# Attention state products in plain fp32, one accumulator for both directions, gate preparation among the first pairs

## Chip, core and metric

The kernel runs on one core of a Trainium2 chip. The metric is device time in microseconds from launch to end. The core has five engines with a queue each, which wait for one another through semaphores: PE (TensorE, matrix products into PSUM; its weight loads are listed as PEld), DVE (VectorE), ACT (ScalarE), POOL (GpSimd) and SP, which here only starts transfers. Each engine works through its queue in order, so an instruction that waits holds up all that stand behind it.

## The reference

One encoder block on x of 1024 tokens by 1024 channels. A conditioned RMS norm gives h; one wide projection of h gives q, k, v, z of a gated linear attention with 4 heads (128 key, 256 value channels), the three inputs of a gMLP branch, and two merge gates. Both branches are projected, weighted by the gates, summed, projected, scaled per channel by `gate` (from the condition c), added to x and normalised.

The attention runs forwards and backwards and sums the two. In chunks, cut to what matters:

```python
b = cumsum(log_a) within a chunk
q_t, k_t, k_end = q * exp(b), k * exp(-b), k * exp(b_last - b)
o_intra = (mask * (q_t @ k_t.T)) @ v
state   = exp(b_last) * state + k_end.T @ v        # carried from chunk to chunk
o       = o_intra + q_t @ state_before_this_chunk
...
o = o_fw + o_bw
o = o * rsqrt(mean(o * o) + EPS) * gla_norm_g
y_gla = (o * silu(z)) @ w_br_gla
```

## The kernel before

All large products are exact to about fp32 by splitting: an operand a becomes ah (a cast to fp32r on ScalarE) and al = a - ah (a subtraction on VectorE, `split_w`, L175 and L176), and a @ b becomes three fp32r products ah bh + ah bl + al bh. Small products (scores, transposes, spreading a row over partitions) are plain fp32.

The stages in order of time: norm and first product (to about 100 us), gMLP's spatial part and the values of heads 0 and 1 (to about 190), the pairs (190 to 575), q and k of head 0, the attention (about 610 to 965) with other dense products between, the projection of the attention's output (`ev_ya`, to about 1000), the output projection.

*Pairs.* `pair` computes two column blocks of the projection by seven half-size products (Strassen-like): 84 matmuls of 128x512. It reads two weight blocks `wa` and `wb` (SP's queue, L566 and L567), forms sums on POOL (L570 to L577), splits them, and evacuates with `evac`. It takes nine 4 KB tiles of ring `w` (`w4`, 12 buffers): wa, wb, their sum, and three split pairs ah/al, sh/sl, bh/bl. There are 20 such pairs: `pair_m` (merge gates, tanh), `pair_uz` (two pairs, gMLP; it holds two buffers of ring `h` for u), `pair_z`. Ring `h` (`ht`, 30 buffers of 4 KB) holds the split activations; during the pairs 12 of its buffers are kept parts of h and 16 the sums of the products.

*Two small jobs among the pairs.* `low_rank_weights` loads and splits the small decay weights (POOL's queue, then ScalarE and VectorE). `residual_gate` builds `gate` from eight 512 KB blocks `wgate` (SP's queue, L672), each accumulated on VectorE (L676); it needs ring `h` for the accumulator `gacc`, for each `wg`, and for `bg`. Both stand behind the tenth of 14 source calls, after `pair_uz(3)` and `pair_m(FB_MA, ta_d, 1)`.

*Attention.* For each head there are four units in the order of `SEQ`: backward over the second half of the tokens, backward over the first, forward over the first, forward over the second. `front` computes decays, q and k with their exponentials and the masked scores (the backward half of the scores stays in `atb`, the forward half is merged into it). `gla_ops` scales, transposes and splits k (keh, kel) and splits q (qth, qtl). `body` walks the unit's four token tiles. `next_state` forms k_end.T @ v in PSUM (`pk`, one bank), adds the decayed state (L854) and splits the new state (L858, L859). `mm3` is the split product. A backward step forms q @ state at once and keeps it in `op` (L902). A forward step forms scores @ v plus q @ state in one accumulator, adds the kept `op` on VectorE (L925) and squares for the norm on ScalarE (L926). After four tiles `rsq` gives the norm factors, VectorE scales (L931), TensorE transposes (L936), VectorE multiplies with z (L938).

Ring `q` (`w1`, 8 buffers of 1 KB) holds the states and their splits, ring `s` (`w2`, 16 buffers of 2 KB) the 128x512 tiles.

*Order.* A planner builds each engine's queue: it walks a modelled timeline and always takes the ready instruction of highest priority; priority follows the source, and what is traced within `tc.high_priority(offset=PRI)` (the attention, L989) is moved 4000 places ahead. So the dense products traced beside a head (`dense_v`, `dense_qk`, `load_gg`, `dense_yb`) fill the places where the attention isn't ready. A tile that finds no free buffer in its ring waits for a release.

Of the kernel before, what the change touches and what calls it, by code (L numbers as in the profile page):

```python
# [44 lines left out]
def hybrid_block_kernel(ctx: ExitStack, tc: tile.TileContext, x, wf, wt, wada, wgate, wvr, wst, alpha, abias,  # L45
# [77 lines left out]
    def w4(shape, dtype, name):  # L123
        return hp.tile(shape, dtype, tag="w", bufs=12, name=nm(name))
# [4 lines left out]
    def w1(shape, dtype, name):  # L129
        return hp.tile(shape, dtype, tag="q", bufs=8, name=nm(name))  # L130
# [556 lines left out]
    pair_m(FB_MB, tb_d, 0)  # L687
    pair_m(FB_MB, tb_d, 1)
    pair_uz(0)
    pair_m(FB_MB, tb_d, 2)  # L690
    pair_uz(1)
    pair_m(FB_MB, tb_d, 3)
    pair_uz(2)
    pair_m(FB_MA, ta_d, 0)
    pair_uz(3)
    pair_m(FB_MA, ta_d, 1)
    low_rank_weights()
    residual_gate()
# [115 lines left out]
    def gla_ops(un):  # L814
# [13 lines left out]
        qth = w2([P, 512], F32R, "qth")  # L828
        qtl = w2([P, 512], F32R, "qtl")
        S.copy(qth, qh)  # L830
        V.tensor_tensor(out=qtl, in0=qh, in1=qth.bitcast(F32), op=ALU.subtract)
        un.update(keh=keh, kel=kel, qth=qth, qtl=qtl)
# [10 lines left out]
    def next_state(un, i, vh, vl, st, last):  # L843

        if last:
            return None
        o = slice(i * P, i * P + P)
        pk = pk_()
        mm3(pk[:, 0:HV], un["keh"][:, o], un["kel"][:, o], vh, vl, True, True)
        s = w1([P, HV], F32, "s")  # L850
        if st is None:
            V.tensor_copy(s, pk[:, 0:HV])
        else:
            V.scalar_tensor_tensor(out=s, in0=st[0], scalar=un["dec"][:, i:i + 1], in1=pk[:, 0:HV], op0=ALU.mult,  # L854
                                   op1=ALU.add)
        sh = w1([P, HV], F32R, "sh")
        sl = w1([P, HV], F32R, "sl")
        S.copy(sh, s)  # L858
        V.tensor_tensor(out=sl, in0=s, in1=sh.bitcast(F32), op=ALU.subtract)  # L859
        return s, sh, sl  # L860
# [4 lines left out]
    opart = {}  # L865
# [18 lines left out]
    def body(h, u):  # L884
# [5 lines left out]
        if not fw:  # L890
            for i in (3, 2, 1, 0):
                t = half * 4 + i
                o = slice(i * P, i * P + P)
                vh, vl = split_v(h, t)
                st = state[0]
                if i == 3:
                    op4 = w4([P, 4, HV], F32, "op")
                op = opart[h, t] = op4[:, i, :]
                if st is not None:
                    po = po_()  # L900
                    mm3(po[:, 0:HV], un["qth"][:, o], un["qtl"][:, o], st[1], st[2], True, True)
                    S.copy(op, po[:, 0:HV])  # L902
                state[0] = next_state(un, i, vh, vl, st, t == 0)
            return
# [5 lines left out]
        so = tiny([P, 4], "so", 2)  # L910
        for i in range(4):
# [4 lines left out]
            op = opart[h, t]  # L916
            pf = po_()
            po = pf[:, 0:HV]
            mm3(po, ath[:, o], atl[:, o], vh, vl, True, st is None)
            if st is not None:  # L920
                mm3(po, un["qth"][:, o], un["qtl"][:, o], st[1], st[2], False, True)
            if t == NT - 1:
                S.copy(op, po)
            else:
                V.tensor_tensor(out=op, in0=po, in1=op, op=ALU.add)  # L925
            S.activation(pf[:, HV:2 * HV], op, AF.Square, accum_out=so[:, i:i + 1])  # L926
            state[0] = next_state(un, i, vh, vl, st, t == NT - 1)
        r = rsq(so, 4, 1.0 / HV)
        for i in range(4):
            op = opart[h, half * 4 + i]  # L930
            V.tensor_scalar(op, op, r[:, i:i + 1], None, op0=ALU.mult)  # L931
        tsl = slice(half * 512, half * 512 + 512)
        for j in range(2):
            pt = po_()
            for i in range(4):
                TE.transpose(pt[:, i * P:(i + 1) * P], opart[h, half * 4 + i][:, j * P:(j + 1) * P], ident)  # L936
# [35 lines left out]
    for h in range(HEADS):  # L972
# [11 lines left out]
        else:  # L984
            if h == 2:
                load_gg()
            for j in range(4 * (h - 2), 4 * (h - 2) + 4):
# [226 lines left out]
```

## Time and profile before

| | |
|---|---|
| median of 3 runs | 1127.99 us (1127.13 to 1130.76) |
| the profiled execution, its own time | 1132.89 us |
| its span, first to last instruction | 1131.2 us |
| mean granted TensorE clock | 0.979 |
| instructions | 14327 |
| DMA traffic | 152.30 MB, mean 135 GB/s |

The page first gives the busy time of each engine and its share of the span, then the span in 40 slices of 28.3 us, a digit of tenths for each. PEclk is the clock that TensorE was granted. The chain is followed back from the last instruction, at each step to what released it. In a group of instructions stand line, engine, operation, output<-input, shapes, count, busy time, mean ns of one, idle time ahead and what ended it. The duration of a matmul overlaps with the next one's; the spacing of the starts is what it costs. A plain fp32 matmul shows as two records.

### The profile page before, as it was taken

How to read it: one execution, taken by the hardware profiler on the slowest of the kernel's cores; microseconds unless marked ns; L12 is line 12 of the kernel's file. 1: busy time of each engine (PE TensorE's matmuls, PEld its weight loads, DVE VectorE, ACT ScalarE, POOL GpSimd, SP SyncE). 2: the span in 40 equal slices, each digit the busy share in tenths (PEclk: the TensorE clock that was granted, in tenths of full speed). 3: DMA queues.
4: the chain of work that ended last, by engine and by line, in shares of the span. 5: the costliest groups of instructions: out<-in, count | busy, mean ns of one | idle time of the engine just before them, and what ended most of it. 6: DMA issues, size and time to landing. Idle time of an engine off the chain costs nothing.

```text
span 1131.2 us, 14327 instructions
## 1 busy us (share of the span) xinstructions
PE 1077.1 (95%) x5348; PEld 902.6 (80%) x5348; DVE 695.1 (61%) x1085; ACT 431.3 (38%) x760; POOL 264.3 (23%) x302
## 2 busy tenths in 40 slices
PE   6889999999999999999999988999899998999997
PEld 4768899888888888777788977988688877788886
DVE  5765577348475757565544569755867795764422
ACT  4453324233324232523324355544635453322222
POOL 2211214333343425433402000200200100021510
PEclk9999999999999999999999989999899997999999
DMA  9531235232323232355245411622642436536012
GB/s 357 202 140 52 103 122 182 80 112 103 121 103 121 103 121 93 137 188 176 103 164 218 159 38 38 211 87 84 230 143 94 147 142 205 175 123 242 19 56 93
DMA packets 55575, 152.30 MB, mean 135 GB/s; under 512 B 7279, under 2 KB 15471, under 8 KB 55506
## 3 DMA queue, kind: packets, MB, share of 16 engines
q1 hardware_dynamic: 40898, 102.42, 25.8%
q0 software_dynamic: 14608, 48.97, 11.8%
q8 instruction: 42, 0.69, 0.3%
q14 instruction: 27, 0.22, 0.1%
HBM read 108.37 MB, written 42.99 MB: 134 GB/s over the span
## 4 chain that ended last, share of the span: by engine, by line
PE 78%; DVE 7%; DMA 5%; ACT 3%; issue 2%; POOL 1%; SPq 0%; POOLq 0%; ACTq 0%; DVEq 0%
PE pd L193 5%; PE pd L194 5%; PE pd L195 5%; PE po L547 4%; PE po L548 4%; PE pd L211 4%; PE pd L212 4%; PE po L549 4%; PE pd L213 4%; PE pd L549 3%; PE pd L548 3%; PE pd L547 3%; PE pk L547 3%; PE pd L511 3%; PE pd L512 3%; PE pk L548 3%
## 5 line engine op out<-in xcount | busy, mean ns | idle before, releaser
L221 POOL TENSOR_TENSOR r<-ms,nhalf 128x1 f32<-128x1 f32 (+1 forms) x24 | 20.8, 866 | 236.4 <-DVE ms L220 234.2
L511 PE MATMUL pd<-tvl,hh 128*128 128x256 f32 (+1 forms) x256 | 74.1, 290 | 0.6 <-DVE tvl L176 0.6
L512 PE MATMUL pd<-tvh,hl 128*128 128x256 f32 (+1 forms) x256 | 74.2, 290 | 0.0
L510 PE MATMUL pd<-tvh,hh 128*128 128x256 f32 (+1 forms) x256 | 74.0, 292 | 0.0
L549 PE MATMUL pd<-hh,al 128*128 128x512 f32 x160 | 63.9, 399 | 3.1 <-DVE al L176 3.1
L547 PE MATMUL pd<-hh,ah 128*128 128x512 f32 x160 | 63.0, 393 | 1.6 <-ACT ah L175 1.6
L548 PE MATMUL pd<-hl,ah 128*128 128x512 f32 x160 | 62.9, 393 | 0.0
L570 POOL TENSOR_TENSOR wsum<-wb 128x512 f32<-128x512 f32 x20 | 26.2, 1311 | 121.5 <-DMA wb<-in_wf 108.3
L176 DVE TENSOR_TENSOR al<-wa,ah 128x1024 fp32r<-128x1024 f32 x20 | 47.2, 2360 | 10.6 <-PE po L548 6.8
L193 PE MATMUL pd<-ggh,wh 128*128 128x512 f32 x128 | 51.5, 402 | 1.4 <-ACT wh L175 1.0
L1045 PE MATMUL pd<-gh,wh 128*128 128x512 f32 x128 | 51.0, 398 | 0.9 <-ACT gh L175 0.5
L1046 PE MATMUL pd<-gh,wl 128*128 128x512 f32 x128 | 50.7, 396 | 0.8 <-DVE wl L176 0.8
L194 PE MATMUL pd<-ggl,wh 128*128 128x512 f32 x128 | 50.9, 399 | 0.0
L195 PE MATMUL pd<-ggh,wl 128*128 128x512 f32 x128 | 50.8, 397 | 0.1
L511 PEld LDWEIGHTS pd<-tvl,hh 128*128 128x128 f32 x256 | 49.7, 194 | 1.0 <-DVE tvl L176 0.8
L193 PE MATMUL pd<-hh,wh 128*128 128x512 f32 x128 | 50.2, 392 | 0.0
L194 PE MATMUL pd<-hl,wh 128*128 128x512 f32 x128 | 50.2, 392 | 0.0
L195 PE MATMUL pd<-hh,wl 128*128 128x512 f32 x128 | 50.1, 391 | 0.0
L510 PEld LDWEIGHTS pd<-tvh,hh 128*128 128x128 f32 x256 | 49.5, 195 | 0.2
L512 PEld LDWEIGHTS pd<-tvh,hl 128*128 128x128 f32 x256 | 49.6, 194 | 0.0
L1047 PE MATMUL pd<-gl,wh 128*128 128x512 f32 x128 | 48.9, 392 | 0.0
L212 PE MATMUL pd<-tl,mh 128*128 128x512 f32 x120 | 46.9, 391 | 0.0
(319 smaller groups left out, 3173.3 us busy)
## 6 DMA issues: line engine op xcount, KB each, us to landing
ws<-in_wf SPq DMA_DIRECT2D x24, 512.0 KB, 5.3
ws<-in_wt SPq DMA_DIRECT2D x22, 512.0 KB, 4.4
wa<-in_wf SPq DMA_DIRECT2D x20, 512.0 KB, 3.8
wb<-in_wf SPq DMA_DIRECT2D x20, 512.0 KB, 4.4
wa<-in_wada SPq DMA_DIRECT2D x16, 512.0 KB, 8.7
xn<-in_x SPq DMA_DIRECT2D x8, 512.0 KB, 8.9
sg_d<-sg POOLq DMA_DIRECT2D x16, 256.0 KB, 2.4
vh_d<-vh SPq DMA_DIRECT2D x32, 128.0 KB, 1.9
```

The costliest lines, as they stand in the source:

```text
L193: TE.matmul(acc, lhsT=hi[:, k, :], rhs=x.hi(k, half), start=(k == 0), stop=False)
L194: TE.matmul(acc, lhsT=hi[:, k, :], rhs=x.lo(k, half), start=False, stop=False)
L195: TE.matmul(acc, lhsT=lo[:, k, :], rhs=x.hi(k, half), start=False, stop=(k == KC - 1))
L212: TE.matmul(acc, lhsT=xh, rhs=lo[:, k % 2, :], start=False, stop=False)
L510: TE.matmul(acc, lhsT=H.hi_t(k, t), rhs=hi, start=(k == 0), stop=False)
L511: TE.matmul(acc, lhsT=H.hi_t(k, t), rhs=lo, start=False, stop=False)
L512: TE.matmul(acc, lhsT=H.lo_t(k, t), rhs=hi, start=False, stop=(k == KC - 1))
L547: TE.matmul(acc, lhsT=a, rhs=xh(k), start=(first and k == 0), stop=False, skip_group_check=not first)
L548: TE.matmul(acc, lhsT=a, rhs=xl(k), start=False, stop=False, skip_group_check=not first)
L549: TE.matmul(acc, lhsT=b, rhs=xh(k), start=False, stop=(k == 3), skip_group_check=not first)
L1045: TE.matmul(acc, lhsT=hi[:, k, :], rhs=GO.hi(k, half), start=(k == 0), stop=False)
L1046: TE.matmul(acc, lhsT=lo[:, k, :], rhs=GO.hi(k, half), start=False, stop=False)
```

## The change

State products: q and the state are no longer split. The backward units keep their states (`sbw`), and the forward step adds both directions' products q @ state, each as one plain fp32 matmul, to the accumulator of scores @ v. The accumulator is copied out by ScalarE and squared from PSUM; the scaling by the norm factor moves from VectorE to ScalarE. `op` becomes one tile of a forward unit.

Order: `residual_gate` stands behind the first pair and `low_rank_weights` behind the third; the pairs are rearranged around them. Of the eight `dense_yb`, three instead of four are traced beside head 2 and five beside head 3. Ring `w` has 11 buffers instead of 12, ring `q` 12 instead of 8.

```diff
     def w4(shape, dtype, name):
-        return hp.tile(shape, dtype, tag="w", bufs=12, name=nm(name))
+        return hp.tile(shape, dtype, tag="w", bufs=11, name=nm(name))
...
     def w1(shape, dtype, name):
-        return hp.tile(shape, dtype, tag="q", bufs=8, name=nm(name))
+        return hp.tile(shape, dtype, tag="q", bufs=12, name=nm(name))
...
     pair_m(FB_MB, tb_d, 0)
+    residual_gate()
     pair_m(FB_MB, tb_d, 1)
+    pair_m(FB_MB, tb_d, 2)
+    low_rank_weights()
     pair_uz(0)
-    pair_m(FB_MB, tb_d, 2)
+    pair_m(FB_MB, tb_d, 3)
     pair_uz(1)
-    pair_m(FB_MB, tb_d, 3)
+    pair_m(FB_MA, ta_d, 0)
     pair_uz(2)
-    pair_m(FB_MA, ta_d, 0)
+    pair_m(FB_MA, ta_d, 1)
     pair_uz(3)
-    pair_m(FB_MA, ta_d, 1)
-    low_rank_weights()
-    residual_gate()
     pair_z(0)
...
         V.tensor_tensor(out=q3, in0=q3, in1=e8[:, :, fa:fa + 1].broadcast_to([P, 4, P]), op=ALU.mult)
-        qth = w2([P, 512], F32R, "qth")
-        qtl = w2([P, 512], F32R, "qtl")
-        S.copy(qth, qh)
-        V.tensor_tensor(out=qtl, in0=qh, in1=qth.bitcast(F32), op=ALU.subtract)
-        un.update(keh=keh, kel=kel, qth=qth, qtl=qtl)
+        un.update(keh=keh, kel=kel)
...
-            V.scalar_tensor_tensor(out=s, in0=st[0], scalar=un["dec"][:, i:i + 1], in1=pk[:, 0:HV], op0=ALU.mult,
+            V.scalar_tensor_tensor(out=s, in0=st, scalar=un["dec"][:, i:i + 1], in1=pk[:, 0:HV], op0=ALU.mult,
                                    op1=ALU.add)
-        sh = w1([P, HV], F32R, "sh")
-        sl = w1([P, HV], F32R, "sl")
-        S.copy(sh, s)
-        V.tensor_tensor(out=sl, in0=s, in1=sh.bitcast(F32), op=ALU.subtract)
-        return s, sh, sl
+        return s
...
                 st = state[0]
-                if i == 3:
-                    op4 = w4([P, 4, HV], F32, "op")
-                op = opart[h, t] = op4[:, i, :]
-                if st is not None:
-                    po = po_()
-                    mm3(po[:, 0:HV], un["qth"][:, o], un["qtl"][:, o], st[1], st[2], True, True)
-                    S.copy(op, po[:, 0:HV])
+                sbw[h, t] = st
                 state[0] = next_state(un, i, vh, vl, st, t == 0)
...
+        op = w4([P, 4, HV], F32, "op")
...
-            op = opart[h, t]
             pf = po_()
             po = pf[:, 0:HV]
-            mm3(po, ath[:, o], atl[:, o], vh, vl, True, st is None)
-            if st is not None:
-                mm3(po, un["qth"][:, o], un["qtl"][:, o], st[1], st[2], False, True)
-            if t == NT - 1:
-                S.copy(op, po)
-            else:
-                V.tensor_tensor(out=op, in0=po, in1=op, op=ALU.add)
-            S.activation(pf[:, HV:2 * HV], op, AF.Square, accum_out=so[:, i:i + 1])
+            inter = [(x["qh"][:, o], y) for x, y in ((units[h, 1 - half], sbw[h, t]), (un, st)) if y is not None]
+            mm3(po, ath[:, o], atl[:, o], vh, vl, True, not inter)
+            for n, (q, y) in enumerate(inter):
+                TE.matmul(po, lhsT=q, rhs=y, start=False, stop=(n == len(inter) - 1))
+            S.copy(op[:, i, :], po)
+            S.activation(pf[:, HV:2 * HV], po, AF.Square, accum_out=so[:, i:i + 1])
...
-            op = opart[h, half * 4 + i]
-            V.tensor_scalar(op, op, r[:, i:i + 1], None, op0=ALU.mult)
+            S.activation(op[:, i, :], op[:, i, :], AF.Copy, scale=r[:, i:i + 1])
...
-                TE.transpose(pt[:, i * P:(i + 1) * P], opart[h, half * 4 + i][:, j * P:(j + 1) * P], ident)
+                TE.transpose(pt[:, i * P:(i + 1) * P], op[:, i, j * P:(j + 1) * P], ident)
...
-            for j in range(4 * (h - 2), 4 * (h - 2) + 4):
+            for j in ((0, 1, 2), (3, 4, 5, 6, 7))[h - 2]:
                 dense_yb(j)
```

More of the change, by code (lines that the diff above doesn't have):

```diff
@@ L864, in hybrid_block_kernel @@
     atb = {}
-    opart = {}
+    sbw = {}
     state = [None]
```

## The prediction

> **What bounds the kernel now.** I read the profile page from its top: busy times, slices, chain by engine.
>
> ```profile
> PE 1077.1 (95%) x5348; PEld 902.6 (80%) x5348; DVE 695.1 (61%) x1085; ACT 431.3 (38%) x760; POOL 264.3 (23%) x302
> PEclk9999999999999999999999989999899997999999
> PE 78%; DVE 7%; DMA 5%; ACT 3%; issue 2%; POOL 1%; SPq 0%; POOLq 0%; ACTq 0%; DVEq 0%
> ```
>
> TensorE is busy 95% of a span of 1131.2 us and carries 78% of the chain. So an edit pays only if it takes work from PE or closes one of its holes. The clock row shows that holes also cost time inside "busy": in some slices the granted clock falls. The stage windows find the holes. Their columns are the stretch, its length, busy time of PE, PEld, DVE, ACT and POOL, granted clock, DMA share and GB/s.
>
> ```profile
> 220.00:440.00 220.00, 219.81 (x963) 179.99 (x962) 133.44 (x144) 75.01 (x105) 81.27 (x89) 1.00 0.30 108
> 460.00:520.00 60.00, 52.59 (x212) 41.17 (x211) 36.19 (x36) 20.72 (x26) 22.61 (x24) 0.94 0.50 170
> 660.00:720.00 60.00, 51.15 (x309) 44.30 (x308) 51.34 (x103) 35.41 (x81) 5.64 (x8) 0.89 0.18 62
> 780.00:820.00 40.00, 33.58 (x159) 26.26 (x158) 34.13 (x66) 23.99 (x48) 8.51 (x13) 0.87 0.53 195
> 820.00:920.00 100.00, 100.00 (x531) 85.80 (x530) 75.17 (x139) 44.31 (x93) 12.98 (x22) 1.00 0.41 147
> 920.00:965.00 45.00, 39.61 (x192) 32.64 (x191) 31.44 (x61) 21.24 (x48) 1.57 (x2) 0.85 0.41 139
> ```
>
> The pairs (220 to 440) have no hole. I price a hole as idle time plus length times the missing clock, a little generously where both fall together. 460 to 520, where low-rank weights and gate are prepared: 7.4 + 60 x 0.06 = 11.0 us. The attention: 8.9 + 6.6 = 15.5 us, 6.4 + 5.2 = 11.6 us, 5.4 + 6.8 = 12.2 us, together 39.3 us. From 820 to 920 the attention lies under dense products and costs nothing beyond its PE time. In the first two of its three holes VectorE is busy 51.3 of 60 us and 34.1 of 40 us: there it, not PE, sets the pace. How the third part of a state's split holds PE, the timeline of 668 to 675 shows (start, length, then in brackets the idle time before and its releaser):
>
> ```profile
> 671.04 0.38 PE L836 MATMUL po<-sl,qth 128*128 128x256 f32 x1 [0.38 <-DVE sl L859]
> 673.35 0.58 PE L836 MATMUL po<-sl,qth 128*128 128x256 f32 x1 [1.09 <-DVE sl L859]
> 675.01 0.42 PE L837 MATMUL po<-sh,qtl 128*128 128x256 f32 x1
> ```
>
> PE waits for the low part of the state, and after two such waits a product of that shape lasts 0.42 us instead of the 0.28 us shown below.
>
> **The state products.** One head has 7 backward and 7 forward products of q with a state, 56 in all. Each is now three fp32r products of 128x256 and becomes one fp32 product. No fp32 product of that width is in the trace; its neighbours are 128 wide (chain of waits, 16 records) and 512 wide (4 records). A plain fp32 product makes two records: L811 runs 64 times and has 128. Three rows of the timeline in a dense stretch give the fp32r spacing.
>
> ```profile
> L811 PE MATMUL pm<-qh,b 128*128 128x128 f32 x128 | 19.1, 287 | 1.9 <-DVE b L806 1.7
> 124.41 1.78 PE pm L444 x16
> 519.68 1.72 PE pm L682 x4
> 175.73 0.28 PE L511 MATMUL pd<-tvl,hh 128*128 128x256 f32 x1
> 175.85 0.28 PE L512 MATMUL pd<-tvh,hl 128*128 128x256 f32 x1
> ```
>
> A record takes 1.78 / 16 = 0.111 us at 128 and 1.72 / 4 = 0.43 us at 512, so 0.215 us at 256 by halving the latter: 0.43 us a product. Three fp32r products at 0.12 us take 0.36 us. The edit **adds** 56 x 0.07 = 3.9 us to PE; the ends are 56 x (0.22 - 0.36) = -7.8 us and 56 x (0.86 - 0.36) = +28 us from the two neighbours, and I stay with the halved row because the two agree with a cost linear in width. The Trainium skill, page "FP8 and Floating Point Precision", section "TensorE Precision Notes", counts four passes for true fp32, which speaks against trading three products for one: at 0.12 us a pass it would be 56 x 0.12 = 6.7 us, an estimate that would move the time by 3 us.
>
> What goes is on the two other engines:
>
> ```profile
> L859 DVE TENSOR_TENSOR sl<-s,sh 128x256 fp32r<-128x256 f32 x56 | 23.5, 419 | 6.5 <-ACT sh L858 5.9
> L831 DVE TENSOR_TENSOR qtl<-qh,qth 128x512 fp32r<-128x512 f32 x16 | 10.9, 683 | 1.3 <-ACT qth L830 1.3
> L925 DVE TENSOR_TENSOR op<-po,op 128x256 f32<-128x256 f32 x28 | 11.7, 422 | 9.0 <-PE po L837 8.9
> L931 DVE TENSOR_SCALAR op<-op,r 128x256 f32<-128x256 f32 x32 | 9.3, 355 | 2.7 <-POOL r L221 2.7
> L858 ACT CAST sh<-s 128x256 fp32r<-128x256 f32 x56 | 22.7, 405 | 40.6 <-DVE s L854 31.0 <-DVE s L852 9.4
> L830 ACT CAST qth<-qh 128x512 fp32r<-128x512 f32 x16 | 10.0, 622 | 1.5 <-PE po L836 1.1 <-PE pk L836 0.3
> L902 ACT COPY op<-po 128x256 f32<-128x256 f32 x28 | 10.2, 371 | 17.4 <-PE po L837 15.9 <-DMA y_d<-tb 1.4
> L926 ACT ACTIVATE po<-op 128x256 f32<-128x256 f32 x32 | 12.3, 386 | 18.1 <-DVE op L925 17.9
> ```
>
> VectorE loses the split of the state, the split of q, the sum of both directions and the norm scaling: 23.5 + 10.9 + 11.7 + 9.3 = 55.4 us. ScalarE loses 22.7 + 10.0 + 10.2 = 42.9 us and gains 28 copies of the accumulator (at 0.371 us, L902: 10.4 us) and 32 scalings (at 0.386 us, L926: 12.4 us): 20 us less. The step from one state to its product also gets shorter by a cast (0.41 us) and a subtraction (0.42 us). What is late next is the state itself (L854), which PE already awaits.
>
> ```profile
> PE pk L835 <- DVE s L854: 4.5, 5, 1.6
> PE po L836 <- DVE sl L859: 2.8, 5, 1.1
> ```
>
> How much returns I work out hole by hole. The same four lines in each hole, one row per line where it is largest:
>
> ```profile
> 660.00:720.00 60.00, 5.02 (x12) 0.89 0.18 62
> 660.00:720.00 60.00, 2.72 (x4) 0.89 0.18 62
> 660.00:720.00 60.00, 2.95 (x7) 0.89 0.18 62
> 660.00:720.00 60.00, 2.35 (x8) 0.89 0.18 62
> ```
>
> Here (L859, L831, L925, L931 in this order) 13.0 us of VectorE's 51.3 us go, out of a hole of 15.5 us. Some of it lay under dense products, so I take 9 us. By the share of the three holes I take 5 of 11.6 us for 780 to 820, where GG's split and late weights also hold PE, and 8 of 12.2 us for 920 to 965, where the length of the chain counts, since the dense products that covered it are used up at 919.5 us:
>
> ```profile
> L193 PE MATMUL pd<-ggh,wh x128: 387/390/796, 801.4 to 919.5; 128*128 128x512 f32 x128
> ```
>
> Together **-22 us**. Its ends are -39 us (all holes closed) and 0.
>
> **Norm scaling on ScalarE.** Four scalings now stand as 4 x 0.386 = 1.5 us between the norm and the transposes, for 4 x 0.355 = 1.4 us on VectorE, and behind whatever ScalarE has begun (a cast like L830's, 0.62 us). Eight units: +1 us, between 0 (covered by dense products) and +5 us. The copy and the square of a tile, both on ScalarE, hold the accumulator's bank as long as the sum and the square did: nothing.
>
> **Gate and low-rank preparation earlier.** 460 to 520 loses 11.0 us.
>
> ```profile
> L676 DVE SCALAR_TENSOR_TENSOR gacc<-wg,gsc,gacc 128x1024 f32<-128x1024 f32 x7 | 11.3, 1620 | 11.6 <-DMA wg<-in_wgate 11.6
> 459.83 5.10 DMA sa<-in_abias
> 481.23 4.45 DMA wg<-in_wgate
> 485.77 1.30 DVE gacc L676
> 487.09 18.28 SPq L672 DMA_DIRECT2D wg<-in_wgate  x4
> 505.42 0.41 SPq L566 DMA_DIRECT2D wa<-in_wf  x1
> ```
>
> The eight weight loads go one after the other, each after the last accumulation (4.45 + 1.30 us). VectorE stands 11.6 us in front of them, and four of them hold SP's queue for 18.28 us with the next pair's weights (L566) behind. The reason is room: of 30 large buffers the activations keep 12 and the four sums 16, so two are left for accumulator and weight. Before the first `pair_uz` this is no different; that is why I do not let the 11 us vanish. What is better there is that a `pair_m` gives VectorE less to do. What is new: u's buffers of `pair_uz(0)` come free only behind gate and low-rank weights, and the wait on the 5.1 us load still stands in ScalarE's queue. I take **-2 us**, between -11 and +8 us.
>
> **Buffers.** A pair uses nine of the 4 KB buffers; 12 become 11.
>
> ```profile
> L175 ACT CAST ah<-wa 128x1024 fp32r<-128x1024 f32 x20 | 21.0, 1050 | 53.5 <-PE po L548 42.7 <-DVE fl L176 9.8 <-PE pd L512 1.1
> PE pd L549 <- DVE al L176: 3.1, 4, 1.6
> ```
>
> The next pair's first cast already waits for a buffer that PE gives up (42.7 us in all), so one buffer fewer delays it further. Five of the pair's seven products remain then as cover, and PE waits only 3.1 us for `al` today. I take **+2 us**; the ends are 0 and one product of 12 matmuls in each of 20 pairs, 55 us (219.81 us for 963 of them, 0.23 us each). In the attention one held buffer goes (`op4` of the backward direction), so it is even there. The 1 KB ring grows to 12 for the seven states kept: nothing. `dense_yb(3)` behind head 2's attention instead of before it: these products are cover of lower rank than the attention in either place, so 0, between -6 and +6 us.
>
> **Sum.** 3.9 - 22 + 1 - 2 + 2 = -17.1 us on the profiled execution's own 1132.89 us (span 1131.2 us): 1115.8 us. That execution lay 4.9 us above the median of the runs, 1127.99 us, so I forecast **1111 us**.
>
> **Rivals.**
> *All of it returns.* If VectorE alone makes the holes, 33 of 39 us and 8 of the gate's 11 us return: 3.9 + 1 - 33 - 8 = -36 us, 1092 us. For it: VectorE at 86% in two holes. Against it: late weights and PE's wait for L854 stay.
> *VectorE's time was cover.* The freed time is spent waiting for the state (4.5 us against 2.8 us for the split). Then only the split's waits and their slow clock return, about 6 us, against 3.9 + 1 + 2 us added: 1128.9 us. Against it: the 51.3 of 60 us.
> *The slow clock has another cause than the stalls.* Then only the idle part of the holes answers, 20.7 of 39.3 us, and of my 22 us some 11 return: 1122 us. For it: the gaps shown ahead of the slow product are only 0.38 and 1.09 us. Against it: it fell in all three holes and nowhere from 820 to 920. The Trainium skill, page "TensorE: Matmul & The Clock Gate", section "HAM oscillation — how this bites in real kernels", speaks for this rival: it lets the clock fall only after a gap of more than about 3.4 us, and these gaps are shorter.
> *Slower: the ring of 11.* In the pair stage, which has no hole now, each pair's `al` comes a release later. At half a product, 1.4 us, in 20 pairs it costs 28 instead of 2 us: 1111 + 26 = 1137 us. It outweighs the rest from 1 us per pair on. For it: the 42.7 us. Against it: five products of cover.
> *The move does not do what it says.* Gate loads wait for one buffer as before, and the 11 us only change place: 1113 us, inside the forecast.
>
> **Chances.** Forecast 0.49 (1100 to 1121 us), clock 0.07, all of it 0.17, cover 0.15, ring 0.12. What a measurement of this kernel tells from no change is about 0.3%, 3.4 us. Faster: 0.49 + 0.07 + 0.17 + 0.04 of the cover case = 0.77; same: the other 0.11; slower: 0.12. The range runs from the case of a full return to beyond that of cover, 1091 to 1132 us; the ring case and half of the full return are left out.
>
> **What would show it.** L859, L831, L925 are gone; the state products are 112 records of 128x256 near 0.215 us apart. VectorE falls to about 640 us, ScalarE to about 411 us. The clock in the attention's holes rises above 0.89, 0.87 and 0.85. Wrong would be: pairs with idle PE before `al`, a hole as deep as 11 us beside the early gate loads, or the same holes with PE waiting on L854.

## The result: slower by 0.7%

The changed kernel took **1137.18 us** (median of 4 runs, 1136.27 to 1138.12), the kernel before, run beside it, 1129.38 us (4 runs, 1127.13 to 1131.16): a ratio of **1.0070** with a 95% interval of 1.0046 to 1.0094. The forecast was 1111 us (1091 to 1132). The profiled execution of the changed kernel took 1136.27 us with a span of 1134.6 us, 3.4 us more than the span before. Of all the runs below one single execution, of order_fp32sep, took 2146 us; its ratio leaves it out.

### The profile after

Busy times and the chain by engine, from the page:

```profile
PE 1073.5 (95%) x5292; PEld 898.3 (79%) x5292; DVE 642.6 (57%) x953; ACT 413.5 (36%) x720; POOL 272.0 (24%) x302
PE 80%; DVE 9%; DMA 4%; ACT 4%; issue 2%; POOL 1%; SPq 0%; POOLq 0%; ACTq 0%; DVEq 0%
```

VectorE and ScalarE fell to what was worked out (642.6 and 413.5 us against 640 and 411), and PE's share of the chain rose by two points. What was meant to go, went; the time did not follow. The windows, in the columns of before:

```profile
220.00:440.00 220.00, 212.38 (x909) 170.88 (x908) 127.22 (x141) 76.26 (x105) 87.92 (x95) 0.98 0.31 110
460.00:520.00 60.00, 58.95 (x258) 47.91 (x257) 37.45 (x42) 18.82 (x27) 24.12 (x26) 1.00 0.37 129
660.00:720.00 60.00, 49.77 (x286) 42.68 (x285) 43.52 (x77) 33.82 (x77) 6.00 (x9) 0.89 0.17 61
780.00:820.00 40.00, 28.51 (x150) 23.40 (x148) 28.13 (x48) 25.63 (x56) 7.69 (x12) 0.87 0.49 171
820.00:920.00 100.00, 98.33 (x498) 83.58 (x499) 68.66 (x114) 42.62 (x89) 12.18 (x20) 0.97 0.41 143
920.00:965.00 45.00, 42.55 (x212) 35.50 (x211) 21.08 (x32) 19.26 (x43) 4.28 (x6) 1.00 0.59 204
```

I price holes as the forecast did, idle time plus length times missing clock. The hole of 460 to 520 went from 11.0 to 1.1 us, and one of 12.0 us (7.6 + 220 x 0.02) opened in 220 to 440, where there was none. In the attention the four rows give 16.8, 16.7, 4.7 and 2.5 us, 40.7 together, where before they gave 15.5, 11.6, 0 and 12.2, 39.3 together. VectorE is no longer near its limit in the first two (43.5 of 60 and 28.1 of 40 us), yet they did not shrink. The longest waits of PE:

```profile
PE pm L811 <- DVE b L806: 9.2, 2, 5.6
PE pk L547 <- DVE u L603: 6.1, 13, 1.0
PE pk L831 <- DVE s L850: 5.4, 8, 1.0
...
PE pm L682 <- DVE gacc L676: 4.0, 1, 4.0
```

The waits for the low part of the state are gone, as they must be. In their place stands L811, the scores of the next unit, waiting for that unit's preparation (1.7 us in two waits before, 9.2 us now). The wait for the state itself (L850, L854 before) grew from 4.5 to 5.4 us. The last column of numbers is the longest single wait. The wait of L682 is that of the gate's products, in the new hole of the pair stage.

One more row for each kernel shows that the attention did get faster. L778 is the first product of each of the 16 units' preparation; the answer for this line gives its first and last start. Before:

```profile
L778 PE MATMUL pm<-RT,ST x16: 389/394/497, 619.0 to 913.4; 128*128 128x512 f32 x16
```

After:

```profile
L778 PE MATMUL pm<-RT,ST x16: 387/394/765, 626.1 to 897.1; 128*128 128x512 f32 x16
...
L193 PE MATMUL pd<-ggh,wh x128: 387/389/737, 816.0 to 943.0; 128*128 128x512 f32 x128
```

From the first to the last preparation it is 271.0 us instead of 294.4, some 23 us less. But it starts 7.1 us later, and the yb products on GG (L193) now run from 816.0 to 943.0 us, where before they ran from 801.4 to 919.5. The attention outran the dense products; PE still had their work left, and the idle time stood elsewhere. A shorter chain in one place was no shorter program.

### The profile page after: what moved, and what is told of

Its sections match the earlier page's. It is cut to its first block, busy times and chain, and to the rows that moved or that the text cites. A ratio compares the mean times of both kernels' runs of the same rounds, so it can differ in the third digit from the quotient of the medians.

```text
span 1134.6 us, 14014 instructions
## 1 busy us (share of the span) xinstructions
PE 1073.5 (95%) x5292; PEld 898.3 (79%) x5292; DVE 642.6 (57%) x953; ACT 413.5 (36%) x720; POOL 272.0 (24%) x302
## 4 chain that ended last, share of the span: by engine, by line
PE 80%; DVE 9%; DMA 4%; ACT 4%; issue 2%; POOL 1%; SPq 0%; POOLq 0%; ACTq 0%; DVEq 0%
PE pd L195 5%; PE pd L194 5%; PE pd L193 5%; PE pd L211 4%; PE pd L212 4%; PE po L549 4%; PE po L547 4%; PE po L548 4%; PE pd L213 4%; PE pk L547 3%; PE pd L549 3%; PE pd L511 3%; PE pd L512 3%; PE pd L510 3%; PE pk L549 3%; PE pk L548 3%
## 5 line engine op out<-in xcount | busy, mean ns | idle before, releaser
L221 POOL TENSOR_TENSOR r<-ms,nhalf 128x1 f32<-128x1 f32 (+1 forms) x24 | 20.5, 854 | 191.6 <-DVE ms L220 133.2
L549 PE MATMUL pd<-hh,al 128*128 128x512 f32 x160 | 62.2, 389 | 0.0
L193 PE MATMUL pd<-ggh,wh 128*128 128x512 f32 x128 | 51.6, 403 | 0.0
L850 DVE SCALAR_TENSOR_TENSOR s<-s,dec,pk 128x256 f32<-128x256 f32 x48 | 22.9, 477 | 50.5 <-PE pk L833 50.3
L193 PE MATMUL pd<-hh,wh 128*128 128x512 f32 x128 | 50.0, 390 | 0.0
L570 POOL TENSOR_TENSOR wsum<-wb 128x512 f32<-128x512 f32 x20 | 29.0, 1448 | 86.3 <-PE po L548 38.3
L175 ACT CAST ah<-wa 128x1024 fp32r<-128x1024 f32 x20 | 21.0, 1051 | 73.0 <-PE po L549 50.2
```

The lines of the kernel that those rows point to most:

```text
L193: TE.matmul(acc, lhsT=hi[:, k, :], rhs=x.hi(k, half), start=(k == 0), stop=False)
L549: TE.matmul(acc, lhsT=b, rhs=xh(k), start=False, stop=(k == 3), skip_group_check=not first)
```

## The experiments

All times are medians; each ratio is to the kernel before, run beside the variant on the same chip, and 1% is 11.3 us. "Changed" is the changed kernel.

| kernel | us | ratio (95%) |
|---|---|---|
| changed | 1137.18 | 1.0070 (1.0046 to 1.0094) |
| order_only | 1128.34 | 0.9970 (0.9954 to 0.9986) |
| ring11 | 1128.54 | 0.9982 (0.9961 to 1.0003) |
| att_only | 1142.58 | 1.0084 (1.0059 to 1.0109) |
| after_yb4 | 1136.46 | 1.0034 (1.0017 to 1.0051) |
| order_fp32sep | 1120.21 | 0.9896 (0.9873 to 0.9919) |
| the same, again | 1117.79 | 0.9884 (0.9862 to 0.9906) |
| after_normv | 1134.14 | 1.0023 (1.0005 to 1.0042) |
| after_w12s14 | 1135.62 | 1.0033 (1.0016 to 1.0049) |
| after_ybw | 1139.74 | 1.0071 (1.0049 to 1.0093) |
| after_sep | 1122.12 | 0.9926 (0.9903 to 0.9948) |
| after_dumb | 1142.92 | 1.0098 (1.0075 to 1.0122) |
| after_dumf | 1143.56 | 1.0106 (1.0085 to 1.0128) |
| sep_s14 | 1127.03 | 0.9960 (0.9939 to 0.9981) |
| after_s18q8 | 1131.49 | 0.9998 (0.9976 to 1.0020) |
| after_s18w10 | 1139.05 | 1.0064 (1.0042 to 1.0086) |
| sep_s18q4 | 1115.61 | 0.9851 (0.9819 to 0.9883) |
| sep_dve | 1127.55 | 0.9968 (0.9950 to 0.9986) |
| after_s18_copyv | 1133.18 | 1.0016 (0.9999 to 1.0033) |

### Which part of the change loses

**order_only**: the kernel before with the changed order of the pair stage.

```
+    pair_m(FB_MB, tb_d, 0)
+    residual_gate()
+    pair_m(FB_MB, tb_d, 1)
+    pair_m(FB_MB, tb_d, 2)
+    low_rank_weights()
     pair_uz(0)
...
-    low_rank_weights()
-    residual_gate()
     pair_z(0)
```

> The kernel before with only the new order of the pair stage (gate and low-rank weights among the first pairs); rings and attention as before. Theory A (the order itself is what lengthens the pair stage: the hole of 460 to 520 closes, and gate and low-rank work open as much or more in 190 to 240): the first state products end some 2 to 5 us later than in the kernel before, and the whole is 1131 to 1135 us against 1129.4. Rival B (the ring of 11 lengthens it): the order alone gives what the forecast said, -2 us or better, 1122 to 1128 us, and no wait of a pair's product on the sum of wa and wb.

**ring11**: `tag="w", bufs=12` becomes 11 in the kernel before.

> The kernel before with only the 4 KB ring cut from 12 to 11. Rival B (the ring makes the start 2.1 us and the pair stage some 4 us longer, with a wait of about 1 us on VectorE's sums in most pairs): 1133 to 1137 us, with the waits of pair products on L603 in it. Theory A (the ring costs nothing by itself): 1128 to 1131 us and none of these waits.

**att_only**: the changed kernel with the order and the yb split of before.

> The changed kernel with the old order of the pair stage and the old split of the yb products, so the attention's part with its rings (11 and 12) alone. Theory A (the pair stage's loss comes from the order; the attention gives a little, 3 to 4 us, because its holes are latency and not VectorE's time): 1124 to 1128 us. Rival B (ring): the attention gives as little, the ring takes 4 to 6 us, 1129 to 1133 us. The forecast's own account (22 us from the attention, eaten up elsewhere by order and yb split): 1112 to 1118 us.

**after_yb4**: in the changed kernel

```
-            for j in ((0, 1, 2), (3, 4, 5, 6, 7))[h - 2]:
+            for j in range(4 * (h - 2), 4 * (h - 2) + 4):
```

> The changed kernel with the yb products split four and four again, so that dense_yb(3) stands ahead of head 2's attention. Theory C (the hole of 780 to 820 grew from 11.6 to 16.7 us because less dense cover stands before it): that hole falls by some 4 us, and the hole of 920 to 965 opens again by some of the 10 us that closed there, 1135 to 1143 us. Rival (the split changes nothing, as the forecast had it): 1135 to 1139 us with all holes as in the changed kernel, 16.8, 16.7 and 2.5 us.

The order alone is a gain of 0.30%, 3.4 us; theory A fell. The ring alone costs nothing that can be told in the whole time (0.9982), though PE's waits on L603 do appear in it (8.4 us in 12 waits); theory B fell too. The loss is in att_only, which holds the attention's edit together with its rings: slower by 0.84%, outside all three expectations. The split of yb changes little: the ratios 1.0034 and 1.0070 have intervals that touch, and after_yb4's holes in the attention are those of the changed kernel to within 0.6 us, so theory C fell.

The ring does cost time where the pair stage is measured by itself. The traces give, from the first product of gMLP's spatial part (L444) to the last start of L549 into `pd`, one of the last pair's products:

| kernel | buffers of ring `w` | order | us |
|---|---|---|---|
| before | 12 | old | 480.1 |
| ring11 | 11 | old | 481.6 |
| att_only | 11 | old | 484.5 |
| order_only | 12 | new | 478.0 |
| after_w12s14 | 12 | new | 478.3 |
| changed | 11 | new | 484.5 |
| after_s18w10 | 10 | new | 489.9 |

In the new order the five profiles with 12 buffers lie at 476.4 to 478.5 us and the ten with 11 at 483.0 to 485.8, so the twelfth buffer is worth some 6 us there. PE's waits on L603 go with it: all of the ten have them (5.4 to 6.4 us in 13 waits), none of the five. With 12 buffers the new order shortens the stage by 2.1 us; with 11 it gains nothing.

Where the order's gain comes from, two windows of order_only show:

```profile
220.00:440.00 220.00, 214.31 (x922) 174.10 (x921) 133.45 (x142) 76.16 (x105) 85.65 (x97) 0.98 0.33 112
460.00:520.00 60.00, 60.00 (x263) 48.78 (x261) 42.16 (x43) 18.30 (x26) 24.19 (x27) 1.00 0.38 131
```

The old hole of 11.0 us is closed, and one of 10.1 us (5.7 + 4.4) stands beside the early gate loads. The hole changed place almost whole, so that in these two stretches only about 1 us is gained. In the same trace the hole of 920 to 965 fell from 12.2 to 7.6 us (4.0 + 3.6), with no edit to the attention; why, I did not trace.

### Product, accumulator, or hand-over

**order_fp32sep**: order_only with a single fp32 product for each state, each direction still in its own accumulator, rings as before.

```
-                    mm3(po[:, 0:HV], un["qth"][:, o], un["qtl"][:, o], st[1], st[2], True, True)
+                    TE.matmul(po[:, 0:HV], lhsT=un["qh"][:, o], rhs=st, start=True, stop=True)
...
-                mm3(po, un["qth"][:, o], un["qtl"][:, o], st[1], st[2], False, True)
+                TE.matmul(po, lhsT=un["qh"][:, o], rhs=st, start=False, stop=True)
```

with L830, L831, L858 and L859 left out.

> The kernel before with the new order of the pair stage, and of the attention's edit only the fp32 state product: no split of q or of the state, but both directions in their own accumulators, sum, norm scaling on VectorE and rings as before. Theory D (the loss sits at the hand-over to the yb products, and comes from where merged accumulator, norm scaling or ring put the casts of GG and of the first yb weights): the product itself is no worse than three, 1118 to 1128 us against 1128 of the order alone. Rival E (the fp32 product or its place in the chain is the loss): 1133 to 1140 us, with the hole of 780 to 820 as large as in the changed kernel.

**after_normv**: `V.tensor_scalar(op[:, i, :], op[:, i, :], r[:, i:i + 1], None, op0=ALU.mult)` in the place of L915.

> The changed kernel with the four norm scalings of a unit on VectorE again. Rival F (norm scaling in ScalarE's queue is what delays the casts of GG and of the first yb weights): first yb product 5 to 10 us earlier than 816 us, 1127 to 1132 us. Theory D with another cause: 1134 to 1139 us, first yb product between 812 and 818 us.

**after_w12s14**: rings `w` 11 to 12, `s` 16 to 14.

> The changed kernel with the 4 KB ring at 12 again, paid for by two buffers of the 2 KB ring (16 to 14). If the ring of 11 delays the loads of GG and of the first yb weights (SyncE's queue stands on them for 30 us from 761 us): the hole of 780 to 820 falls by some 5 us and the pair products no longer wait for L603, 1127 to 1133 us. If not: 1134 to 1139 us.

**after_ybw**: ahead of GG's loads

```
             if h == 2:
+                yb_w[0] = fm_weights(FB_YB)
                 load_gg()
```

> The changed kernel with one move: the first yb product's weights are loaded and split ahead of GG's loads instead of behind them. Theory D (the yb products start late because their first weights are cast at 814.28 us, behind seven casts of GG): first yb product 7 to 12 us earlier, the hole of 780 to 820 from 16.7 to 8 us or less, 1125 to 1131 us. If GG itself is what is late: the wait moves from the weights to GG's casts and the time stays at 1134 to 1139 us.

order_fp32sep is 0.74% faster than order_only, 0.86% in its second run: the fp32 product is a gain of 8 to 10 us, and rival E fell. Scaling on VectorE again is 0.47% better than the changed kernel but only 0.11% better than after_yb4, within what these intervals can tell; its first yb product still starts at 815.8 us, so rival F fell. after_w12s14 is 0.37% better than the changed kernel, less than expected of the ring, but it holds two edits of opposite sign: its pair stage is 6.2 us shorter and the waits on L603 are gone, while two 2 KB buffers fewer cost after_sep 0.34% (below). The changed kernel with the ring at 12 and nothing else was not run.

after_ybw shows why theory D was wrong. Its windows:

```profile
780.00:820.00 40.00, 34.53 (x171) 27.49 (x169) 29.54 (x49) 24.78 (x53) 7.71 (x12) 0.91 0.55 191
820.00:920.00 100.00, 95.39 (x475) 80.19 (x476) 67.18 (x112) 41.49 (x85) 12.48 (x21) 0.97 0.41 143
920.00:965.00 45.00, 38.49 (x186) 31.49 (x185) 19.21 (x29) 20.00 (x45) 3.67 (x5) 0.92 0.58 192
```

The hole aimed at did fall, from 16.7 to 9.1 us, as expected. But the next two grew from 4.7 to 7.6 and from 2.5 to 10.1 us: 26.8 us instead of 23.9 in the three. The dense product done earlier was missing as cover later, and the time did not move (1.0071).

### The shared accumulator alone

**fp32sep_again** repeats order_fp32sep, whose profile is read from this run.

> The same kernel as order_fp32sep, for a profile in the usual state and for its time beside the three others of this call: 1117 to 1123 us. By theory G (below) its backward units have no waits of 3 us or more of the scores (L811) for VectorE's product with k (L806), since state products fill these places.

**after_sep**: the changed kernel with only the shared accumulator undone.

```
-            for n, (q, y) in enumerate(inter):
-                TE.matmul(po, lhsT=q, rhs=y, start=False, stop=(n == len(inter) - 1))
-            S.copy(op[:, i, :], po)
-            S.activation(pf[:, HV:2 * HV], po, AF.Square, accum_out=so[:, i:i + 1])
+            if st is not None:
+                TE.matmul(po, lhsT=un["qh"][:, o], rhs=st, start=False, stop=True)
...
+                V.tensor_tensor(out=op, in0=po, in1=op, op=ALU.add)
+            S.activation(pf[:, HV:2 * HV], op, AF.Square, accum_out=so[:, i:i + 1])
```

and in the backward units the product with a copy to `op`, as in order_fp32sep.

> The changed kernel with only the shared accumulator undone: each direction has its own again (copy by ScalarE, sum by VectorE), state products stay single fp32 ones, norm scaling stays on ScalarE, rings stay 11 and 12, the order and the yb split stay. Theory G (the shared accumulator takes the backward state products out of the backward units, where PE waits anyway for the next unit's preparation, and puts them into the forward units, where PE is needed): 1120 to 1127 us. Rival H (ring of 11 and norm scaling on ScalarE make up the loss, the shared accumulator is innocent): 1133 to 1138 us.

**after_dumb** and **after_dumf**: `TE.matmul(po_()[:, 0:HV], ...)` 28 times, in the backward and in the forward units.

> The changed kernel with 28 more state products whose result nobody reads, one at each state of the backward units, where the kernel before had its backward products. 28 x 0.43 = 12 us of PE work. Theory G (PE is idle there anyway): 0 to +4 us, 1136 to 1141 us. Rival (PE's work is what counts everywhere): +10 to +13 us, 1147 to 1150 us.

> The same 28 unread products, placed in the forward units ahead of the copies. Theory G: they cost what the moved products cost, 7 to 13 us more than the changed kernel, and at least 5 us more than the same products in the backward units. Rival (place does not matter): the same time as with the products in the backward units, within 3 us.

after_sep settles which edit loses: it is 1.44% faster than the changed kernel, 16 us (1.1 to 1.8% by the two intervals), with the same 112 records of fp32 products, the same order, rings, split and scaling, and although VectorE adds the two directions again. Rival H fell. Its attention windows:

```profile
660.00:720.00 60.00, 50.83 (x324) 44.87 (x323) 43.20 (x80) 34.28 (x77) 4.36 (x6) 0.97 0.16 53
...
780.00:820.00 40.00, 34.84 (x172) 27.56 (x171) 33.06 (x58) 24.41 (x48) 8.40 (x13) 0.91 0.54 192
820.00:920.00 100.00, 99.71 (x514) 85.18 (x514) 69.89 (x119) 44.94 (x93) 12.53 (x22) 1.00 0.46 155
920.00:965.00 45.00, 44.62 (x224) 37.65 (x222) 21.77 (x36) 16.61 (x38) 3.12 (x4) 1.00 0.50 171
```

11.0 + 8.8 + 0.3 + 0.4 = 20.5 us of holes, half of the changed kernel's 40.7. That is the difference of the two spans (1134.6 and 1118.3 us) and a little more. So the holes can be closed, and the shared accumulator keeps them open.

The reason I gave for it, theory G, fell by the unread products: in the forward units they cost about what they cost in the backward ones (1.0106 and 1.0098). Against the changed kernel that is 3 to 4 us by the ratios and some 6 us by the medians, for 12 us of PE's work: it is partly hidden in either place. The rival, that the place does not matter, stood; after_dumb's 1142.92 us lies between its own two expectations.

### What the shared accumulator keeps

With it, `qh` of both backward units must live until the forward units have read it: two buffers of the 2 KB ring (`s`) that before went free with each unit. The ring also feeds the next units' preparation (`e`, `b`, `qh`). The timeline at the tenth preparation (head 2, second backward unit) shows what that does. In the changed kernel, L778 on PE, then ScalarE:

```profile
772.89 0.39 PE L778 MATMUL pm<-RT,ST 128*128 128x512 f32 x1
...
774.66 0.37 ACT L910 COPY op<-po 128x256 f32<-128x256 f32 x1 [3.85 <-PE po L909]
...
780.34 0.37 ACT L910 COPY op<-po 128x256 f32<-128x256 f32 x1 [3.81 <-PE po L909]
...
786.03 0.37 ACT L910 COPY op<-po 128x256 f32<-128x256 f32 x1 [2.47 <-PE po L909]
...
786.69 0.59 ACT L780 ACTIVATE e<-pm 128x512 f32<-128x512 f32 x1
```

In after_sep:

```profile
775.14 0.39 PE L778 MATMUL pm<-RT,ST 128*128 128x512 f32 x1
...
775.57 0.60 ACT L780 ACTIVATE e<-pm 128x512 f32<-128x512 f32 x1 [1.96 <-PE pm L778]
```

L780, which writes the new `e`, follows its product after 13.8 us in the one and 0.4 us in the other. No semaphore wait stands ahead of it in the changed kernel: the planner put it behind three tiles' copies in ScalarE's queue, and those wait for PE. In the kernel before this preparation was late as well, by 11.9 us:

```profile
770.17 0.40 PE L778 MATMUL pm<-RT,ST 128*128 128x512 f32 x1
...
782.06 0.60 ACT L780 ACTIVATE e<-pm 128x512 f32<-128x512 f32 x1 [1.60 <-PE po L837]
```

There the split of q took two more 2 KB buffers in every unit. Whether the ring is the cause can be tried from both sides.

**sep_s14**: after_sep with `s` 16 to 14. **after_s18q8**: changed, `s` 16 to 18, `q` 12 to 8. **after_s18w10**: changed, `s` 16 to 18, `w` 11 to 10. **sep_s18q4**: order_fp32sep with `s` 16 to 18, `q` 8 to 4.

> after_sep (separate accumulators) with the 2 KB ring cut from 16 to 14 and nothing else. Theory S (the shared accumulator keeps q of both backward units, two 2 KB buffers, until the forward units are done; the preparation of the next head's second backward unit then lacks a buffer, and its first ScalarE step, L780, comes 14 us behind its product L778 instead of 0.4 us): the two buffers taken away here do the same, 1128 to 1137 us against 1122, and L780 of the tenth preparation comes 5 us or more behind L778. Rival (the buffers are not scarce, the shared accumulator loses by its own chain of products): 1120 to 1125 us and no delay of L780.

> The changed kernel with two 2 KB buffers more (16 to 18), paid for with four of the 1 KB ring (12 to 8, the seven kept states and one). Theory S: the delay of the tenth L780 falls from 13.8 to below 3 us and the time from 1137 to 1122 to 1130 us. Rival: 1135 us or more, the more so as the states now wait for a buffer.

> The same two buffers more, paid for with one of the 4 KB ring (11 to 10), states' ring at 12. Theory S: delay of the tenth L780 below 3 us, the attention shorter by 8 to 14 us, less what a ring of 10 costs the pair stage (some 2 to 6 us): 1124 to 1134 us. Rival: 1137 us or more.

> The fastest kernel so far (single fp32 state products, separate accumulators, new order) with the 2 KB ring at 18, paid for with four of the eight 1 KB buffers, since a state now needs one instead of three. By theory S no preparation there waits for a 2 KB buffer any more (tenth L780 0.4 us behind L778), so nothing is left to gain: 1114 to 1121 us.

In sep_s14 the delay comes back:

```profile
775.95 0.39 PE L778 MATMUL pm<-RT,ST 128*128 128x512 f32 x1
...
784.25 0.58 ACT L780 ACTIVATE e<-pm 128x512 f32<-128x512 f32 x1
```

and in after_s18q8 it goes:

```profile
768.57 0.39 PE L778 MATMUL pm<-RT,ST 128*128 128x512 f32 x1
...
769.00 0.60 ACT L780 ACTIVATE e<-pm 128x512 f32<-128x512 f32 x1 [2.51 <-PE pm L778]
```

The delay follows the ring both ways: 8.3 us with two buffers fewer, 0.4 us with two more. The time follows it in part. Two buffers fewer cost after_sep 0.34%, 4 us (about as much as the two intervals can tell apart; the least of what theory S gave, 1128 to 1137, was just missed); two buffers more bring the changed kernel 0.72%, 8 us, even with four state buffers fewer (1131.5, just above 1122 to 1130). after_s18w10 missed its expectation and gave the rival's time (1139.05): the 4 KB buffer given up takes back what the two bring. Against after_s18q8 its pair stage is 6.9 us longer and the ratios differ by 7.5 us, though the delay of L780 is gone there too (0.4 us). So the short 2 KB ring explains 4 to 8 of the 16 us.

How the delay turns into time is not shown. In after_s18q8, whose attention starts 4.4 us earlier, the hole of 780 to 820 is as large as in the changed kernel, 9.8 + 6.8 = 16.6 us:

```profile
780.00:820.00 40.00, 30.25 (x147) 23.86 (x147) 30.77 (x53) 24.80 (x53) 7.51 (x12) 0.83 0.55 198
```

Of the four stretches only 820 to 920 closed (from 4.7 us to 0).

sep_s18q4 has the lowest time of the study, **1115.61 us, 0.9851 (0.9819 to 0.9883)**, 1.5% below the kernel before and inside its expectation; its interval overlaps that of fp32sep_again, so two more buffers gained nothing there that can be told.

### Does VectorE's time count, and what is left

**sep_dve**: order_fp32sep with VectorE's removed work given back where nobody reads it.

```
+            V.tensor_tensor(out=dmy, in0=qh[:, n * HV:n * HV + HV], in1=qh[:, 0:HV], op=ALU.subtract)
...
+        V.tensor_tensor(out=dmy, in0=s, in1=s, op=ALU.subtract)
         return s
```

> The kernel with single fp32 state products and separate accumulators (order_fp32sep) to which VectorE's removed work is given back as unread subtractions: one of 128x256 behind each of the 56 states and two of 128x256 in each unit, off the chain, about 56 x 0.42 + 32 x 0.42 = 37 us of VectorE; the 1 KB ring goes from 8 to 7. No 2 KB buffer is added. The forecast's theory (VectorE sets the pace in the first two holes): the gain goes, 1126 to 1130 us against 1118 to 1120. Rival S (the gain came from the two 2 KB buffers that each unit no longer takes, and from the shorter step from a state to its product): 1117 to 1123 us, tenth L780 still 0.4 us behind L778.

**after_s18_copyv**: after_s18q8 with `V.tensor_copy(op[:, i, :], po)` in the place of L910.

> after_s18q8 (the changed kernel with two 2 KB buffers more) with the 32 copies out of the shared accumulator on VectorE instead of ScalarE, where they stand between product and square. If the rest of the loss against separate accumulators (1131 against 1122 us) is ScalarE's longer queue in the forward units: 1123 to 1128 us. If it is the missing backward state products while PE waits for the next unit's preparation (3.7 us ahead of L811): 1129 to 1134 us.

The groups of the added work in sep_dve (busy time, mean ns of one, idle time before):

```profile
L855 DVE TENSOR_TENSOR dmy<-s 128x256 f32<-128x256 f32 x56 | 23.6, 421 | 0.8
...
L830 DVE TENSOR_TENSOR dmy<-qh 128x256 f32<-128x256 f32 x32 | 13.5, 422 | 0.3
```

37.1 us of work on no chain but VectorE's own queue cost 0.72 to 0.84%, 8 to 10 us: the whole gain of the fp32 product, while the tenth L780 stayed 0.4 us behind its product. Rival S fell: what the fp32 product gains is VectorE's time, though that engine is busy only 62% of the span. Where it is gained is not where the forecast had it. fp32sep_again:

```profile
660.00:720.00 60.00, 50.67 (x329) 45.89 (x329) 47.51 (x91) 30.35 (x67) 6.92 (x10) 0.91 0.23 78
780.00:820.00 40.00, 32.55 (x153) 25.64 (x152) 34.44 (x63) 21.27 (x38) 8.36 (x13) 0.87 0.56 204
920.00:965.00 45.00, 44.63 (x224) 37.84 (x223) 25.66 (x46) 13.90 (x29) 2.58 (x3) 1.00 0.52 176
```

sep_dve:

```profile
780.00:820.00 40.00, 30.51 (x148) 23.24 (x147) 37.53 (x74) 20.59 (x36) 8.14 (x13) 0.91 0.58 204
920.00:965.00 45.00, 41.17 (x199) 33.42 (x198) 29.12 (x57) 13.03 (x29) 2.68 (x3) 0.96 0.54 177
```

The first two holes are 14.7 and 12.7 us without the added work, 14.6 (row at the end of this text) and 13.1 with it, and 15.5 and 11.8 in order_only: no difference to speak of. The third is 0.4, 5.6 and 7.6 us, and from the first preparation to the last it is 278.4, 285.3 and 295.3 us. VectorE's time thus lengthens the attention, and it shows at the end, where the dense products are used up. That VectorE makes the first two holes is not shown.

after_s18_copyv gained nothing (1.0016 against 0.9998), so ScalarE's longer queue is not what the shared accumulator still costs. What remains after the ring, 8 us or more, is not settled. One place of it can be seen, at the end of the first head's cover. Changed:

```profile
681.43 2.05 PE L811 MATMUL pm<-qh,b 128*128 128x128 f32 x8 [3.64 <-DVE b L806]
```

after_sep:

```profile
680.94 1.13 PE L811 MATMUL pm<-qh,b 128*128 128x128 f32 x8 [0.99 <-DVE b L806]
```

Both come 8.1 or 8.2 us behind their L778 (673.27 and 672.87 us). In after_sep backward state products fill part of that time; in the changed kernel PE has none there, stands for 3.64 us, and the eight records behind it take 2.05 instead of 1.13 us. In after_s18q8 the wait is as long, so the 2 KB ring is not its cause:

```profile
677.03 2.05 PE L811 MATMUL pm<-qh,b 128*128 128x128 f32 x8 [3.66 <-DVE b L806]
```

That such places make up the remaining 8 us was only argued.

## Why the prediction was wrong

Chaining the ratios, each step against the one before: order -0.30% (-3.4 us), fp32 product -0.80% (-9, mean of its two runs), rings, norm scaling and yb split together +0.36% (+4), shared accumulator +1.44% (+16): +0.70%. Each step is known to 0.2 to 0.3%, so the third is barely clear of nothing. The changed kernel was not run again beside the later variants.

- **State products, +3.9: right.** In a dense stretch after the change:

```profile
842.46 0.59 PE L909 MATMUL po<-s,qh 128*128 128x256 f32 x2
842.71 0.58 PE L195 MATMUL pd<-ggh,wl 128*128 128x512 f32 x1
843.12 0.39 PE L193 MATMUL pd<-ggh,wh 128*128 128x512 f32 x1
```

  A state product's two records and one wide product take 0.66 us from the first start to the third line's. Wide products follow each other there at 0.23 us, which leaves 0.43 us, the halved row. The four passes of the Trainium skill ("FP8 and Floating Point Precision", section "TensorE Precision Notes") would give 4 x 0.12 = 0.48 us, an estimate; the trace lies below it.
- **Attention, -22: the step that failed.** It took all of VectorE's 55.4 us for one gain, and set the price of the shared accumulator at nothing, in two sentences: its bank is held no longer than before ("nothing"), and the 1 KB ring grows for the seven states kept ("nothing"). The list of what the shared sum keeps had left out q: two 2 KB buffers for two units' length, in the ring from which every preparation takes three. The two halves of the edit have opposite signs. The shared accumulator lost 16 us, of which the ring explains 4 to 8; the rest is open. The fp32 product brought 9 us net, and by VectorE's time, as forecast (sep_dve), but not by the 9 and 5 us of the first two holes, which it left as they were: the four stretches hold 27.8 us of holes in fp32sep_again and 34.9 in order_only, and nearly all of the difference is the third. Of the signs of being wrong, the hole beside the early gate loads came, and PE's longer wait for the state came in part.
- **Holes one by one.** The third closed (12.2 to 2.5 us) by more than the 8 us forecast, in part by the order alone (7.6 us in order_only), while 780 to 820 and 820 to 920 grew from 11.6 and 0 to 16.7 and 4.7. after_ybw shows such a trade again. Adding three holes' gains was wrong in kind: a dense product done in one hole is missing as cover behind it.
- **Norm scaling, +1.** L915 takes 0.495 us, not the 0.386 us assumed (1.7 us for four). With ring and split it is in the +4 us. after_normv, which takes it back, is 5 us faster than the changed kernel, but after_yb4 is 4 us faster by an edit that changes little, so what belongs to the scaling is not settled.
- **Gate earlier, -2: right in sign and nearly in size** with a ring of 12 (-3.4; -2.1 in the pair stage). That the 11 us would change place and not vanish was right; the reason given for the gain, less work for VectorE beside a `pair_m`, was not tested. With the ring of 11 the pair stage gains nothing from the order (484.5 us in att_only and in the changed kernel).
- **Ring of 11, +2: too small.** In the new order it costs some 6 us of the pair stage. 1137 us is the slower rival's number, but by luck: it asked for 28 us of the ring, and its sign, idle PE ahead of `al`, did not appear. PE waits on L603 instead.
- **yb split, 0:** the ratios with and without it have touching intervals.
- **The clock.** It stood at 0.89 in 660 to 720 before, with no single gap over 1.18 us there, and at 0.97 in after_sep with gaps up to 1.43 us:

```profile
676.61 1.62 PE L811 MATMUL pm<-qh,b 128*128 128x128 f32 x6 [1.18 <-DVE b L806]
```

  That is the longest of before. The changed kernel, at 0.89 as well, has the gap of 3.64 us, from 677.8 to 681.4 us, but there the clock had fallen ahead of it:

```profile
676.78 0.58 PE L831 MATMUL pk<-vh,keh 128*128 128x256 f32 x1 [0.94 <-DVE s L850]
...
676.00:677.00 1.00, 0.22 (x1) 0.22 (x2) 1.00 (x3) 0.00 (x0) 0.00 (x0) 0.83 0.00 0
677.00:678.00 1.00, 0.79 (x3) 0.49 (x3) 0.97 (x2) 0.00 (x0) 0.00 (x0) 0.50 0.00 0
```

  The Trainium skill's rule ("TensorE: Matmul & The Clock Gate", section "HAM oscillation — how this bites in real kernels"), a gap of more than about 3.4 us, thus agrees with neither kernel. What lowers the clock in these holes stays open.

## What to carry to other kernels

When a sum over two passes moves into one accumulator, write down everything that the first pass must then keep, and from which ring the next unit's first step takes its buffer; here two short-lived buffers that became long-lived cost 4 to 8 us. Measure a smaller ring in the stage that uses it, since the whole time can hide it. Predict and measure such an edit apart from the one that it comes with: here the product alone was worth -0.8% and the sum +1.4%. And count holes under shared cover once, as a total, since a hole that is closed hands its cover's absence on to the next.

## What was not expected of the hardware

37.1 us of VectorE work that nothing waits for cost 8 to 10 us of time with that engine busy only 62%: the average hides an engine that is short of time in the attention (53.2 of 60 us in the window below, of sep_dve).

```profile
660.00:720.00 60.00, 49.00 (x323) 43.91 (x323) 53.16 (x110) 30.55 (x67) 8.54 (x9) 0.94 0.23 75
```

ScalarE's scaling of a 128x256 tile by a column took 0.495 us, its square of the same tile 0.386 us.
